# One ring of score row tiles, longer loads, and the first lists made between row tiles, in an argmax, gather and scatter kernel

## The chip, the cores and the metric

One core of a Trainium2 chip. The metric is the time of one execution in microseconds (us), as the device reports it; a profiled execution of the same program has a span some 2 us shorter. All runs quoted here are in the fast state, at full clock.

## The reference

```python
B, S, H = (8, 2048, 2560)          # scores: B x S x S, values: B x S x H, float32
...
best_j   = np.argmax(scores, axis=2)
...
gathered = values[b_idx, best_j, :].copy()
out = np.zeros_like(values)
np.add.at(out, (b_idx, best_j, slice(None)), gathered)
```

For each batch, row j of the output is values[j] times the number of score rows whose largest element is in column j. So only the counts are needed: rows with count 1 are copied, rows with count 0 are zeroed, rows with a higher count are gathered, scaled and scattered. With random scores about 37% are of the first kind, 37% of the second.

## The kernel before

VectorE finds the column of the maximum of every score row (two passes over 128 x 2048 elements, 4.6 us a row tile, 16 row tiles a batch) and turns columns into one-hot tiles from which TensorE makes the counts. From the counts VectorE makes three lists of row numbers. GpSimd issues one indirect transfer per 128 list entries; entries past the end of a list are dropped. SyncE loads the scores, 2 rows per partition (2 MB) at a time:

```python
    R = 2
    ...
    NV = 6                        # staging slots of H elements for the gathered rows
    NX = NV * H // (R * S)        # score tiles of two rows that fit into that room
    NB = 7
    ...
    spool = ctx.enter_context(tc.tile_pool(name="spool", bufs=NB))
    ...
    vbig = ctx.enter_context(nc.sbuf_tensor([P, NV * H], FP32))
...
        for u in range(NT // R):                      # count_steps: one batch of scores
            x = b * NT // R + u
            if x < 2 * (NX + NB) and x % (NX + NB) < NX:
                x %= NX + NB
                s_tile = vbig[:, x * R * S:(x + 1) * R * S]     # early: also in the staging room
            else:
                s_tile = spool.tile([P, R * S], FP32, name="s_tile")[:]
            ...
            for r in range(R):
                ...
                nc.vector.max(out=mx[:], in_=rows)
                nc.vector.max_index(out=am[:, g, :], in_max=mx[:], in_values=rows)
                if g < G - 1:
                    yield
...
        first = 6 if b < 2 else 4                     # value_steps: the lists of one batch
        for t in range(first):
            copy_once(t)
        ...                                           # zero and many lists; three yields in between
        def gathers():
            for k in range(MCAP):
                v = stage()
                gather(v, mi[:, k:k + 1])
                nc.scalar.activation(out=v, in_=v, func=Copy, bias=0.0, scale=mc[:, k:k + 1])
                ...
        ...
        if b == 0:
            zeros(range(nz))          # each zero scatter also issues one of the copies left
            for _ in range(10):
                yield
            gathers()
        else:
            ...
        for k in range(MCAP):
            scatter(staged[k], mi[:, k:k + 1], ...)
...
        for b in range(B):
            for _ in count_steps(b, cnt_ps):
                next(pending, None)   # one step of the lists of the batch before
            ...
            pending = value_steps(b, cnt_ps)
            if b < 2:
                for _ in range(4):    # batches 0 and 1: lists in one go
                    next(pending)
```

Of the kernel before, what the change touches and what calls it, by code (L numbers as in the profile page):

```python
# [8 lines left out]
FP32 = mybir.dt.float32  # L9
# [5 lines left out]
P = 128  # L15
# [21 lines left out]
def kernel(  # L37
# [6 lines left out]
    nc = tc.nc  # L44
    B, S, S2 = scores.shape
    _, _, H = values.shape
    assert S == S2
    NT = S // P
    BIG = float(1 << 24)
    R = 2  # L50
    G = 4
    NV = 6
    NX = NV * H // (R * S)
    NB = 7
    NM = NT // 2
    NE = 16
    LE = P // NE
# [7 lines left out]
    last_row = nc.gpsimd.to_reg(B * S - 1)  # L65

    consts = ctx.enter_context(tc.tile_pool(name="consts", bufs=1))
    spool = ctx.enter_context(tc.tile_pool(name="spool", bufs=NB))
    small = ctx.enter_context(tc.tile_pool(name="small", bufs=3))
    fin = ctx.enter_context(tc.tile_pool(name="fin", bufs=2))  # L70
    ohp = ctx.enter_context(tc.tile_pool(name="ohp", bufs=1))
# [44 lines left out]
    zero1 = consts.tile([P, 1], FP32)  # L116
# [2 lines left out]
    zrow = ctx.enter_context(nc.sbuf_tensor([P, H], FP32))  # L119
    nc.scalar.copy(zrow[:], zero1[:].to_broadcast([P, H]))  # L120

    vbig = ctx.enter_context(nc.sbuf_tensor([P, NV * H], FP32))
    nc.scalar.copy(vbig[:, NX * R * S:NV * H], zero1[:].to_broadcast([P, NV * H - NX * R * S]))

    ones_i = ctx.enter_context(nc.sbuf_tensor([P, B * NT], INT32))
    zero_i = ctx.enter_context(nc.sbuf_tensor([P, B * NT], INT32))
# [30 lines left out]
            in_=v, in_offset=None, bounds_check=B * S - 1, oob_is_err=False))  # L157

    vslot = [0]

    def stage():
        v = vbig[:, vslot[0] * H:(vslot[0] + 1) * H]
        vslot[0] = (vslot[0] + 1) % NV
        return v

    def count_steps(b, cnt_ps):

        am = None
        for u in range(NT // R):
            x = b * NT // R + u  # L170
            if x < 2 * (NX + NB) and x % (NX + NB) < NX:
                x %= NX + NB
                s_tile = vbig[:, x * R * S:(x + 1) * R * S]
            else:
                s_tile = spool.tile([P, R * S], FP32, name="s_tile")[:]
            rows_in = scores[b, u * R * P:(u + 1) * R * P, :].rearrange("(p r) s -> p (r s)", r=R)

            parts = R if b == u == 0 else 1
            for r in range(parts):
                part = slice(r * R * S // parts, (r + 1) * R * S // parts)  # L180
                nc.sync.dma_start(out=s_tile[:, part], in_=rows_in[:, part])
            if u * R % G == 0:
                am = small.tile([P, G, 8], U32, name="am")
            for r in range(R):
                g = (u * R + r) % G
                rows = s_tile[:, r * S:(r + 1) * S]
                mx = small.tile([P, 8], FP32)
                nc.vector.max(out=mx[:], in_=rows)  # L188
                nc.vector.max_index(out=am[:, g, :], in_max=mx[:], in_values=rows)  # L189
                if g < G - 1:  # L190
                    yield
            if (u + 1) * R % G == 0:
                lo = small.tile([P, G], U32)
                nc.vector.tensor_single_scalar(out=lo[:], in_=am[:, :, 0], scalar=P - 1, op=ALU.bitwise_and)  # L194
                hi = small.tile([P, G], U32)
                nc.vector.tensor_single_scalar(out=hi[:], in_=am[:, :, 0], scalar=7, op=ALU.logical_shift_right)  # L196
                oh_lo = small.tile([P, G, P], BF16)
                nc.vector.tensor_tensor(  # L198
                    out=oh_lo[:], in0=lo[:].unsqueeze(2).to_broadcast([P, G, P]),
                    in1=lane_f[:].unsqueeze(1).to_broadcast([P, G, P]), op=ALU.is_equal)  # L200
                oh_hi = small.tile([P, G, NT], BF16)
                nc.vector.tensor_tensor(  # L202
                    out=oh_hi[:], in0=hi[:].unsqueeze(2).to_broadcast([P, G, NT]),
                    in1=lane_f[:, 0:NT].unsqueeze(1).to_broadcast([P, G, NT]), op=ALU.is_equal)
                for g in range(G):
                    t = (u + 1) * R - G + g
                    nc.tensor.matmul(out=cnt_ps[:], lhsT=oh_lo[:, g, :], rhs=oh_hi[:, g, :],  # L207
                                     start=(t == 0), stop=(t == NT - 1))
                yield

    def level_engines(rank):

# [59 lines left out]
    def value_steps(b, cnt_ps):  # L272
# [14 lines left out]
                nc, out_flat[:, :], values[b, t * P:(t + 1) * P, :], one_i[:, t:t + 1], last_row))  # L287


        first = 6 if b < 2 else 4  # L290
        for t in range(first):
            copy_once(t)

# [22 lines left out]
        if b == B - 1:  # L316
# [9 lines left out]
            out=oh[:], in0=lo[:].unsqueeze(2).to_broadcast([P, NT, P]),  # L326
# [4 lines left out]
            out=ez[:], in0=hi[:, 0, :].unsqueeze(2).to_broadcast([P, NT, NT]),  # L331
# [3 lines left out]
            out=em[:], in0=hi[:, 1, :].unsqueeze(2).to_broadcast([P, NT, NM]),  # L335
# [6 lines left out]
        for t in range(NT):  # L342
            nc.tensor.matmul(out=l_ps[:], lhsT=oh[:, t, :], rhs=put[:, t, :], start=(t == 0), stop=(t == NT - 1))  # L343
        yield
        yield

        mi = many_i[:, b * NM:(b + 1) * NM]
        mc = many_c[:, b * NM:(b + 1) * NM]
# [10 lines left out]
# [4 lines that stand above are left out]
                nc.scalar.activation(out=v, in_=v, func=mybir.ActivationFunctionType.Copy, bias=0.0,  # L363
                                     scale=mc[:, k:k + 1])
                staged.append(v)
                if rest:
                    copy_once(rest.pop(0))

        def zeros(columns):
            for k in columns:  # L370
                scatter(zrow[:], zi[:, k:k + 1], free_running)
                if rest:
                    copy_once(rest.pop(0))
# [3 lines left out]
        if b == 0:  # L377
            zeros(range(nz))

            for _ in range(10):  # L380
                yield
            gathers()
        else:
            gathers()
            zeros(range(ZHEAD))
# [9 lines left out]
    with tc.manual_schedule(engines={ET.PE, ET.DVE, ET.Activation, ET.SP}):  # L395
        pending = iter(())
        for b in range(B):
            cnt_ps = psum_c.tile([P, NT], FP32)
            for _ in count_steps(b, cnt_ps):
                next(pending, None)  # L400
            for _ in pending:
                pass
            pending = value_steps(b, cnt_ps)
            if b < 2:
                for _ in range(4):
                    next(pending)
        for _ in pending:
            pass
        full = fin.tile([1, 2], FP32)
        nc.vector.tensor_reduce(out=full[:, 0:1], in_=tots[0:1, 0, 0:B - 1], op=ALU.max, axis=mybir.AxisListType.X)  # L410
        nc.vector.tensor_reduce(out=full[:, 1:2], in_=tots[0:1, 1, :], op=ALU.max, axis=mybir.AxisListType.X)
        over = fin.tile([1, 3], FP32)
        nc.vector.tensor_single_scalar(out=over[:, 0:1], in_=full[:, 0:1], scalar=float(ZCAP * P), op=ALU.is_gt)
        nc.vector.tensor_single_scalar(out=over[:, 1:2], in_=full[:, 1:2], scalar=float(MCAP * P), op=ALU.is_gt)
        nc.vector.tensor_single_scalar(out=over[:, 2:3], in_=most[0:1, :], scalar=float(ZLAST * LE), op=ALU.is_gt)
        over_i = fin.tile([1, 1], INT32)
        nc.vector.tensor_reduce(out=over_i[:], in_=over[:], op=ALU.max, axis=mybir.AxisListType.X)
# [3 lines left out]
    with tc.If(more > 0):  # L421
# [20 lines left out]
        for b in range(B):  # L442
            for k in range(MCAP, NM):
# [3 lines left out]
                with tc.issue_after(last.ins):  # L447
                    scaled = nc.gpsimd.tensor_scalar(
                        out=zrow[:], in0=zrow[:], scalar1=many_c[:, i:i + 1], scalar2=None, op0=ALU.mult)
# [37 lines left out]
```

## Time and profile before

| | before |
|---|---|
| time, median of 3 runs (4 by the time of the comparison) | 828.03 us (828.37) |
| span of the profiled run | 826.9 us |
| bytes moved, of them score loads | 347.04 MB, 134.22 MB |
| VectorE busy, until | 679.3 us, about 700 us |
| mean rate of the transfers over the span | 420 GB/s |
| rate at 90 to 110 us, and at 150 to 171 us | 367 GB/s, 426 GB/s |

The lines to read are in the prediction below. The point of them: VectorE and the DMA engines are both full, but VectorE ends 127 us before the kernel does, so the end is set by bytes over rate. Only time in which the transfers move less than some 427 GB/s can be won. The place aimed at is at 90 to 110 us, when VectorE makes all lists of batch 0 in one go, no score tile comes free, and the load queue runs dry.

### The profile page before, as it was taken

The numbers are of one execution on the slowest core, as the hardware profiler recorded it, in microseconds if no ns is written. First come the engines' busy times: TensorE is split into PE (matmuls) and PEld (weight loads), VectorE is DVE, ScalarE is ACT, GpSimd is POOL, SyncE is SP. The second block draws the span as 40 slices with busy tenths as digits, with TensorE's granted clock in tenths as the row PEclk, the third lists the DMA queues.
The fourth block names the chain that finished last, engine by engine and source line by source line (L and its number), as shares of the span: only waits on it lengthen the run. The fifth ranks groups of instructions, "written<-read, shape, count | busy, mean of one in ns | idle before, by whom it ended". The sixth has DMA issues, their size and how long they took to land.

```text
span 826.9 us, 2079 instructions
## 1 busy us (share of the span) xinstructions
PE 14.7 (2%) x273; PEld 14.2 (2%) x273; DVE 679.3 (82%) x794; ACT 103.0 (12%) x43; POOL 274.1 (33%) x277
## 2 busy tenths in 40 slices
PE   0000000000000000000000000000000000000000
PEld 0000000000000000000000000000000000000000
DVE  7999999999999999999999999999999996000000
ACT  3000000501210001220002300002200220230230
POOL 0000643157021160052330151511425356346442
DMA  9999999999999999999999999999999999999997
GB/s 380 430 426 430 372 423 422 425 411 422 423 425 428 428 427 430 425 427 427 429 424 426 426 430 430 422 429 426 427 426 423 424 427 422 425 424 424 422 427 295
DMA packets 48112, 347.04 MB, mean 420 GB/s; under 512 B 19014, under 2 KB 19014, under 8 KB 19014
## 3 DMA queue, kind: packets, MB, share of 16 engines
q0 software_dynamic: 38736, 212.67, 62.0%
q1 hardware_dynamic: 9360, 134.22, 38.2%
q14 instruction: 14, 0.11, 0.0%
q8 instruction: 2, 0.03, 0.0%
HBM read 354.42 MB, written 300.15 MB: 792 GB/s over the span
## 4 chain that ended last, share of the span: by engine, by line
DVE 43%; DMA 18%; issue 17%; POOL 11%; another core or an unknown queue 8%; PE 0%; POOLq 0%
DVE am L189 19%; DVE mx L188 18%; DMA vbig<-in_values_dram,many_i 14%; POOL out_dram L33 6%; DMA out_dram<-vbig,many_i 4%; POOL out_dram L155 4%; POOL vbig L150 2%; DVE oh_lo L198 1%; DVE oh L325 1%; DMA vbig<-in_scores_dram 1%; DVE lo L194 0%; DVE oh_hi L202 0%; PE l_ps L343 0%; DVE put L340 0%
## 5 line engine op out<-in xcount | busy, mean ns | idle before, releaser
L189 DVE FIND_INDEX8 am<-mx,s_tile 128x8 uint32<-128x2048 f32 x116 | 265.0, 2285 | 0.0
L188 DVE MAX8 mx<-s_tile 128x8 f32<-128x2048 f32 x116 | 264.3, 2278 | 0.0
L363 ACT ACTIVATE vbig<-vbig,many_c 128x2560 f32<-128x2560 f32 x40 | 96.8, 2426 | 692.7 <-DMA vbig<-in_values_dram,many_i 658.5
L33 POOL DMA_INDIRECT out_dram<-in_values_dram,ones_i x128 | 132.3, 1033 | 152.3 <-DVE m L296 114.3
L155 POOL DMA_INDIRECT out_dram<-vbig,many_i x40 | 39.3, 983 | 239.1 <-ACT vbig L363 236.3
L150 POOL DMA_INDIRECT vbig<-in_values_dram,many_i x40 | 41.9, 1048 | 126.8 <-DMA out_dram<-vbig,many_i 79.2
L155 POOL DMA_INDIRECT out_dram<-zrow,zero_i x61 | 59.5, 976 | 18.8 <-issue 18.8
L188 DVE MAX8 mx<-vbig 128x8 f32<-128x2048 f32 x12 | 27.3, 2279 | 4.8 <-DMA vbig<-in_scores_dram 4.8
L189 DVE FIND_INDEX8 am<-mx,vbig 128x8 uint32<-128x2048 f32 x12 | 27.4, 2284 | 0.0
L198 DVE TENSOR_TENSOR oh_lo<-lo,lane_f 128x512 bf16<-128x512 uint32 x32 | 22.3, 696 | 0.4
L325 DVE TENSOR_TENSOR oh<-lo,fill_f 128x2048 f16<-128x2048 uint32 x8 | 18.3, 2292 | 0.3
L207 PE MATMUL cnt_ps<-oh_hi,oh_lo 128*128 128x16 bf16 x128 | 8.2, 174 | 579.0 <-DVE oh_hi L202 529.4
L207 PEld LDWEIGHTS <-oh_lo 128*128 128x128 bf16 x128 | 8.4, 105 | 578.8 <-DVE oh_lo L198 577.8
L189 DVE MATCH_VALUE_LOAD am<-mx,s_tile 128x8 f32 x116 | 10.7, 92 | 4.0
L202 DVE TENSOR_TENSOR oh_hi<-hi,lane_f 128x64 bf16<-128x64 uint32 x32 | 7.0, 217 | 0.0
L194 DVE TENSOR_SCALAR lo<-am 128x4 uint32<-128x4 uint32 x32 | 5.8, 181 | 1.1
L343 PE MATMUL l_ps<-put,oh 128*128 128x32 f16 x128 | 4.7, 188 | 68.8 <-DVE put L340 68.8
L343 PEld LDWEIGHTS <-oh 128*128 128x128 f16 x128 | 4.7, 104 | 69.9 <-DVE oh L325 59.6
L196 DVE TENSOR_SCALAR hi<-am 128x4 uint32<-128x4 uint32 x32 | 5.4, 170 | 0.0
L351 DVE TENSOR_SCALAR e<-l_ps 128x32 f32<-128x32 f32 x8 | 1.5, 187 | 3.1 <-PE l_ps L343 3.1
L330 DVE TENSOR_TENSOR ez<-hi,lane_f 128x256 f16<-128x256 uint32 x8 | 3.3, 418 | 0.0
L340 DVE TENSOR_TENSOR put<-ez,row_f 128x256 f16<-128x256 f16 x8 | 3.3, 417 | 0.0
(91 smaller groups left out, 61.3 us busy)
## 6 DMA issues: line engine op xcount, KB each, us to landing
s_tile<-in_scores_dram SPq DMA_DIRECT2D x58, 2048.0 KB, 12.0
vbig<-in_scores_dram SPq DMA_DIRECT2D x5, 2048.0 KB, 37.3
vbig<-in_scores_dram SPq DMA_DIRECT2D x2, 1024.0 KB
out_dram<-in_values_dram,ones_i POOLq DMA_INDIRECT x128
out_dram<-zrow,zero_i POOLq DMA_INDIRECT x61
vbig<-in_values_dram,many_i POOLq DMA_INDIRECT x40, 33.0
out_dram<-vbig,many_i POOLq DMA_INDIRECT x40, 59.1
```

What stands on the lines that cost most here:

```text
L33: return eng.add_instruction(ins)
L150: note(nc.gpsimd.indirect_dma_start(out=v, out_offset=None, in_=values_flat[:, :], in_offset=bass.IndirectOffsetOnAxis(ap=idx, axis=0), bo ...
L155: note(nc.gpsimd.indirect_dma_start(out=out_flat[:, :], out_offset=bass.IndirectOffsetOnAxis(ap=idx, axis=0), in_=v, in_offset=None, bound ...
L188: nc.vector.max(out=mx[:], in_=rows)
L189: nc.vector.max_index(out=am[:, g, :], in_max=mx[:], in_values=rows)
L194: nc.vector.tensor_single_scalar(out=lo[:], in_=am[:, :, 0], scalar=P - 1, op=ALU.bitwise_and)
L198: nc.vector.tensor_tensor(out=oh_lo[:], in0=lo[:].unsqueeze(2).to_broadcast([P, G, P]), in1=lane_f[:].unsqueeze(1).to_broadcast([P, G, P]) ...
L202: nc.vector.tensor_tensor(out=oh_hi[:], in0=hi[:].unsqueeze(2).to_broadcast([P, G, NT]), in1=lane_f[:, 0:NT].unsqueeze(1).to_broadcast([P, ...
L207: nc.tensor.matmul(out=cnt_ps[:], lhsT=oh_lo[:, g, :], rhs=oh_hi[:, g, :], start=(t == 0), stop=(t == NT - 1))
L325: nc.vector.tensor_tensor(out=oh[:], in0=lo[:].unsqueeze(2).to_broadcast([P, NT, P]), in1=fill_f[:].unsqueeze(1).to_broadcast([P, NT, P]), ...
L343: nc.tensor.matmul(out=l_ps[:], lhsT=oh[:, t, :], rhs=put[:, t, :], start=(t == 0), stop=(t == NT - 1))
L363: nc.scalar.activation(out=v, in_=v, func=mybir.ActivationFunctionType.Copy, bias=0.0, scale=mc[:, k:k + 1])
```

## The change

Its intent: keep the transfers full around the first lists. All score tiles become single row tiles in one room (7 in the staging room for the first two turns, 14 behind it, 21 where there were 20). Loads take up to 4 rows per partition where places lie side by side, 1 row for tiles 36 to 41, 2 rows for tiles 42 to 63. For batch 0, only the list of single rows is made at once, all 16 copies are issued first, and the other lists are made between row tiles of batch 1.

```diff
-    R = 2
+    R = 4
...
-    NX = NV * H // (R * S)
-    NB = 7
+    NX = NV * H // S
+    NB = 14
...
+    room = ctx.enter_context(nc.sbuf_tensor([P, NV * H + NB * S], FP32))
...
+    turn = NX + NB
...
+    def place(x):
+        return NV * H + (x % turn - NX if x < 2 * turn else (x - 2 * turn) % NB) * S
...
+    while x < B * NT:
+        n = 1
+        most_n = 1 if x < 2 or 2 * turn - 6 <= x < 2 * turn else 2 if x < 4 or 2 * turn <= x < 4 * NT else R
+        while n < most_n and (x + n) % NT and place(x + n) == place(x) + n * S:
+            n += 1
+        loads[x] = n
+        x += n
...
-        for u in range(NT // R):
...
+        for t in range(NT):
+            x = b * NT + t
+            if x in loads:
+                n = loads[x]
+                nc.sync.dma_start(out=room[:, place(x):place(x) + n * S], in_=...)
...
-        first = 6 if b < 2 else 4
+        first = (NT, 6, 4)[min(b, 2)]
...
         yield
-        yield
+        if b > 0:
+            yield
...
-            for _ in range(10):
+            while tiles[0] < turn + NX:
                 yield
...
...
-            if b < 2:
-                for _ in range(4):
-                    next(pending)
+            for _ in range((1, 4, 0)[min(b, 2)]):
+                next(pending)
```

More of the change, by code (lines that the diff above doesn't have):

```diff
@@ L67 @@
     consts = ctx.enter_context(tc.tile_pool(name="consts", bufs=1))
-    spool = ctx.enter_context(tc.tile_pool(name="spool", bufs=NB))
     small = ctx.enter_context(tc.tile_pool(name="small", bufs=3))
@@ L120 @@
     nc.scalar.copy(zrow[:], zero1[:].to_broadcast([P, H]))
-    vbig = ctx.enter_context(nc.sbuf_tensor([P, NV * H], FP32))
-    nc.scalar.copy(vbig[:, NX * R * S:NV * H], zero1[:].to_broadcast([P, NV * H - NX * R * S]))
+    room = ctx.enter_context(nc.sbuf_tensor([P, NV * H + NB * S], FP32))
+    nc.scalar.copy(room[:, 0:NV * H - NX * S], zero1[:].to_broadcast([P, NV * H - NX * S]))
+    turn = NX + NB
+    def place(x):
+        return NV * H + (x % turn - NX if x < 2 * turn else (x - 2 * turn) % NB) * S
+    loads, x = {}, 0
+    while x < B * NT:
[5 more added lines that the diff above has]
+        x += n
     ones_i = ctx.enter_context(nc.sbuf_tensor([P, B * NT], INT32))
@@ L159 @@
     vslot = [0]
+    tiles = [0]
     def stage():
-        v = vbig[:, vslot[0] * H:(vslot[0] + 1) * H]
+        v = room[:, vslot[0] * H:(vslot[0] + 1) * H]
         vslot[0] = (vslot[0] + 1) % NV
@@ L168, in count_steps @@
         am = None
-        for u in range(NT // R):
-            x = b * NT // R + u
-            if x < 2 * (NX + NB) and x % (NX + NB) < NX:
-                x %= NX + NB
-                s_tile = vbig[:, x * R * S:(x + 1) * R * S]
-            else:
-                s_tile = spool.tile([P, R * S], FP32, name="s_tile")[:]
-            rows_in = scores[b, u * R * P:(u + 1) * R * P, :].rearrange("(p r) s -> p (r s)", r=R)
-            parts = R if b == u == 0 else 1
-            for r in range(parts):
-                part = slice(r * R * S // parts, (r + 1) * R * S // parts)
-                nc.sync.dma_start(out=s_tile[:, part], in_=rows_in[:, part])
-            if u * R % G == 0:
-                am = small.tile([P, G, 8], U32, name="am")
-            for r in range(R):
-                g = (u * R + r) % G
-                rows = s_tile[:, r * S:(r + 1) * S]
-                mx = small.tile([P, 8], FP32)
-                nc.vector.max(out=mx[:], in_=rows)
-                nc.vector.max_index(out=am[:, g, :], in_max=mx[:], in_values=rows)
-                if g < G - 1:
-                    yield
-            if (u + 1) * R % G == 0:
+        for t in range(NT):
+            x = b * NT + t
+            if x in loads:
+                n = loads[x]
+                nc.sync.dma_start(out=room[:, place(x):place(x) + n * S],
+                                  in_=scores[b, t * P:(t + n) * P, :].rearrange("(p r) s -> p (r s)", r=n))
+            g = t % G
+            if g == 0:
+                am = small.tile([P, G, 8], U32, name="am")
+            rows = room[:, place(x):place(x) + S]
+            mx = small.tile([P, 8], FP32)
+            nc.vector.max(out=mx[:], in_=rows)
+            nc.vector.max_index(out=am[:, g, :], in_max=mx[:], in_values=rows)
+            if g == G - 1:
                 lo = small.tile([P, G], U32)
@@ L204, in count_steps @@
                     in1=lane_f[:, 0:NT].unsqueeze(1).to_broadcast([P, G, NT]), op=ALU.is_equal)
-                for g in range(G):
-                    t = (u + 1) * R - G + g
-                    nc.tensor.matmul(out=cnt_ps[:], lhsT=oh_lo[:, g, :], rhs=oh_hi[:, g, :],
-                                     start=(t == 0), stop=(t == NT - 1))
-                yield
+                for k in range(G):
+                    nc.tensor.matmul(out=cnt_ps[:], lhsT=oh_lo[:, k, :], rhs=oh_hi[:, k, :],
+                                     start=(t == G - 1 and k == 0), stop=(t == NT - 1 and k == G - 1))
+            tiles[0] = x + 1
+            yield
     def level_engines(rank):
@@ L344, in value_steps @@
         yield
-        yield
+        if b > 0:
+            yield
         mi = many_i[:, b * NM:(b + 1) * NM]
```

## The prediction

> **What bounds the kernel now.** I read the page from its top: engine shares first, then the strip of slices.
>
> ```profile
> PE 14.7 (2%) x273; PEld 14.2 (2%) x273; DVE 679.3 (82%) x794; ACT 103.0 (12%) x43; POOL 274.1 (33%) x277
> ...
> DVE  7999999999999999999999999999999996000000
> ...
> DMA  9999999999999999999999999999999999999997
> ```
>
> Two things are full at once. VectorE runs without a break until about 700 us and then stops; the 16 DMA engines are in the top band in every slice but the last. So I asked what is left after VectorE has ended, and what the queues moved in all.
>
> ```profile
> DMA packets 48112, 347.04 MB, mean 420 GB/s; under 512 B 19014, under 2 KB 19014, under 8 KB 19014
> ...
> q0 software_dynamic: 38736, 212.67, 62.0%
> q1 hardware_dynamic: 9360, 134.22, 38.2%
> ```
>
> The score loads (q1) are 134.22 MB; the GpSimd transfers (q0: copies of rows that occur once, zero rows, gathers and scatters of rows that occur often) are 212.67 MB. After 700 us only q0 is left, at full speed: from 700 to 810 us it moved 46.68 MB at 424 GB/s and a DMA share of 1.01 to 1.03. A batch has 212.67/8 = 26.6 MB of such work, so when VectorE ends nearly two batches of it are in arrears. A VectorE that ended earlier would therefore not end the kernel earlier: the transfer engines set the time. The chain of waits starts with VectorE (am and mx, 37%) because it follows the last release at each step; it does not show that the transfers were full meanwhile.
>
> The end is thus bytes over rate, plus what the DMA engines lost. At the 427 GB/s of 300 to 600 us, 347.04 MB take 812.7 us; the span is 826.9, so 14.2 us are lost. Where, the table of 10 us stretches shows (last two columns: DMA share, GB/s; before those the engines' busy time):
>
> ```profile
> 0.00:10.00 10.00, 0.00 (x0) 0.00 (x0) 4.34 (x8) 6.26 (x3) 1.09 (x8) 1.00 0.84 329
> 80.00:90.00 10.00, 0.45 (x6) 0.39 (x6) 9.24 (x27) 0.00 (x0) 3.36 (x3) 1.00 1.01 429
> 90.00:100.00 10.00, 0.59 (x16) 0.58 (x16) 8.87 (x14) 0.00 (x0) 7.87 (x8) 1.00 0.93 325
> 100.00:110.00 10.00, 0.00 (x0) 0.00 (x0) 9.90 (x9) 0.00 (x0) 7.56 (x9) 1.00 1.01 409
> 180.00:190.00 10.00, 0.00 (x0) 0.00 (x0) 9.93 (x7) 0.00 (x0) 7.56 (x9) 1.00 1.01 386
> 810.00:820.00 10.00, 0.00 (x0) 0.00 (x0) 0.00 (x0) 0.00 (x0) 1.50 (x2) 1.00 0.95 390
> 820.00:830.00 10.00, 0.00 (x0) 0.00 (x0) 0.00 (x0) 0.00 (x0) 0.00 (x0) 1.00 0.16 56
> ```
>
> In time at 427 GB/s: the start 2.3 us (10 x (1 - 329/427)), the hole at 90 to 110 us 2.8 us (2.4 + 0.4), the dip at 180 about 1.0, the end (4.45 MB in the last 16.9 us, which need 10.4) 6.5 us. These make 12.6 of the 14.2 us; the rest is spread thin.
>
> The hole is what the change aims at. At 84 us the counts of batch 0 are ready; VectorE then makes all lists of batch 0 in one go, from 84.9 to 93.2 us, with the 2.29 us one-hot tile and a 1.02 us wait for PE in it, and finishes no score tile. The load queue waits for exactly that:
>
> ```profile
> SPq L181 <- DVE am L189: 45.8, 4, 18.6
> SPq L181 <- DVE hi L196: 29.5, 4, 9.0
> ```
>
> (time in all up to 110 us, times, longest). The longest, 18.6 us, is the load of rows 36 and 37, which needs both row tiles 16 and 17: 93.2 us plus two tiles of 4.6 us is 102.4, and the next load is issued at 102.8. What was queued ran dry at about 92 us: q1 has 26 packets in 90 to 100 us. Meanwhile q0 had six copies, one each 1.28 us, of which only some 37% of the 128 rows are moved (128 copies of 128 rows for a share of rows of 1/e under random counts: about 0.48 MB each, an estimate), so 0.48/1.28 = 376 GB/s at most.
>
> **What the Trainium skill says.** "DMA: Bandwidth & Descriptors", section "Where 436 GB/s comes from", puts the ceiling at 435.2 GB/s. The trace agrees: score loads alone, 10 to 80 us, ran at 429 GB/s, 98.5% of it, so there is no faster stage to be had. Its section "Issuing engines are not separate DMA queues" says that transfers of all issuers interleave on the same 16 engines; agreed, the shares 62.0% and 38.2% add to 100%. Its section "Queues, rings and completion order" says that each engine takes turns among its queues packet by packet; a bigger packet would give the score queue a larger turn. No run here shows it yet. Its section "Why small descriptors are slow" names a fixed cost per packet. My own reading from the trace: alone, a 16 KB score packet took 16 x 70 / 1831 = 612 ns (2055 packets less 224 small ones), and a 10 KB row in the tail 16 x 110 / 4557 = 386 ns. The slope is 226 ns for 6144 B, 27.2 GB/s per engine, leaving about 10 ns per packet.
>
> **The change, part by part.** No arithmetic goes: the VectorE program has 653 rows in both builds, GpSimd issues the same kinds and numbers of transfers, and the bytes are the same.
>
> *Loads.* Before: 65 loads (63 of 2 rows, 2 of 1), 65 x 128 = 8320 data packets, plus 16 small ones each, the 9360 of the page. After, worked from the code: 48 loads (20 of 4, one of 3, 18 of 2, 9 of 1). The 4-row form is not only late: tiles 4 to 35 have it (with one of 1 and one of 3), then six of 1, eleven of 2 up to tile 63, then 4 and 2. Packets are 48 x 144 = 6912. 17 x 128 = 2176 data packets saved x 10.4 ns / 16 engines = 1.4 us.
>
> *Start.* The first two loads are 1 row as before, so the first wait of VectorE (4.8 us) stays. At 2.45 us per row tile (1.05 MB at 429), tiles 4 to 7 land as one at 5.9 + 7 x 2.45 = 23 us; VectorE took its fifth tile at 26.2. No new wait. Ring of 21: tiles 21 to 24 need tiles 0 to 3 (done at 25), 32 to 35 need tile 14 (done at 78.9) and the queue would run dry at 5.9 + 31 x 2.45 = 81.8; tight but enough. Tile 36 needs 15, done at 83.5, dry at about 91.6.
>
> *The hole.* After: at 84 us VectorE makes only the list of single rows (to the first yield, 1.9 us), then tile 16, then the big lists, then tile 17. Tile 37 can be loaded once 16 is done, at about 91.5, and no longer needs 17. GpSimd has 16 copies to issue at once, 86 to 106.6 us, then 7 zero scatters. So q0 gets 376 GB/s of work and q1 at least a row tile per 5 to 10 us on top, more than 427 together. Lost bytes come back: at most 2.8 us. But of that only 0.7 us is idle share (0.93 in ten us); the rest is slow packets, since the copies carry many dropped rows (585 small q0 packets in 90 to 100 us), and those must be processed whenever they come. I count 2.0.
>
> *Later for batch 0.* Gathers need the value room free: before from 122.1 us (row tile 21), now from tile 22 on, about 127 us. By 115.6 us q0 will have been given 16 x 0.48 + 7 x 1.03 = 14.9 MB and can't have drained more than some 8 of it. No gap. VectorE saves about 1 us of PE wait, which is worth nothing at the end.
>
> *Batch 1 and the tail.* The four steps at once remain for batch 1, so the dip at 180 stays; the last batch and the 6.5 us of the end are untouched.
>
> *Against it.* Four-row loads come every 19 us or more and leave q0 alone between. q0 alone ran at 424, mixed 427: 0.7% over some 60 us of more separate running is 0.4 us.
>
> Sum: 828.0 - 2.0 - 1.4 + 0.4 = 825.0 us.
>
> **Rivals.** (a) *VectorE starves on big loads.* A ring of 14 with 4 in flight leaves 10 tiles, 46 us of VectorE work; a 2 MB load beside q0 took 12.0 us to land, so 4 MB some 24. Even if a few waits of 5 us came, the arrears of q0 at 700 us would absorb them. Time: 825 to 827. (b) *Bigger turns of the score queue starve q0*, so that scaled rows come late and GpSimd's chain is longer. For it: gathers took 33.0 us to land, scatters 59.1, and GpSimd waited 236 us on ACT. Against it: loads are paced by VectorE, so their share over 20 us can't grow. If gaps of 1 us came in each of six batches: 829 to 831. (c) *The hole is only displaced*: sixteen thin copies in a row are processed at the same slow rate, or tile 38 is late instead. Then only the packets count: 826.5 to 828. (d) *Longer packets stream better than my 10 ns*: with 20 ns, 822 to 823.
>
> **Range and chances.** (c) and (b) set the high end, (d) with the whole hole returned (828.0 - 2.8 - 2.8 = 822.4) and some thin losses repaired the low end: 820.5 to 828.5. Two per cent are 16.6 us, more than all losses together (14.2 us), so faster by that is nearly excluded; slower would need 7 MB of new idle time where 50 MB of arrears stand by.
>
> **What would show it.** Right: at 90 to 110 us over 415 GB/s, no load wait of 18 us; 6912 q1 packets and q1's share down to about 38.0%; VectorE still ending near 700; a tail after 810 as before. Wrong: a DMA share under 0.95 somewhere between 110 and 800 us (GpSimd's chain), waits of VectorE on score loads beyond the first, or a rate in score-only stretches well off 429 (longer packets behave otherwise).

## The result

| | before | changed |
|---|---|---|
| time, median (4 runs each) | 828.37 us | 827.43 us |
| changed over before | | 0.9988, 95% interval 0.9971 to 1.0005 |
| span of the profiled run | 826.9 us | 825.6 us |
| packets on the load queue | 9360 | 6912 |

It is inside the predicted range, but the forecast gain of 3.0 us came out as 0.9 us. A second set of five runs (label d3_changed_again below) gave 0.9986, interval 0.9973 to 0.9999, so a gain of some 1 us is likely real. Ratios here are the mean time of one kernel's fast runs over that of the other's of the same rounds, so they are not quite the ratio of the medians. As the kernel before varies by about 1 us from set to set, kernels are compared below by their ratios to it, multiplied by 828.

The pages of the changed kernel that answer to the first lines in the prediction:

```profile
DVE  7999999999999999999999999999999996000000
...
DMA  9999999999999999999999999999999999999997
...
q0 software_dynamic: 38736, 212.67, 62.1%
q1 hardware_dynamic: 6912, 134.22, 38.1%
```

Packets and bytes are as worked out (q0 is GpSimd's queue, q1 the load queue). Nothing in the strips tells the two kernels apart. The table of stretches does (last two columns: DMA share, GB/s). First the kernel before:

```profile
90.00:110.00 20.00, 0.59 (x16) 0.58 (x16) 18.77 (x22) 0.00 (x0) 15.43 (x16) 1.00 0.97 367
110.00:150.00 40.00, 0.51 (x8) 0.53 (x8) 39.66 (x33) 4.43 (x2) 11.85 (x12) 1.00 1.01 424
150.00:171.00 21.00, 0.25 (x4) 0.26 (x4) 20.76 (x21) 7.71 (x4) 3.90 (x4) 1.00 1.02 426
171.00:200.00 29.00, 1.31 (x26) 1.24 (x26) 27.07 (x47) 0.64 (x1) 21.67 (x20) 1.00 1.01 410
```

and the changed kernel:

```profile
90.00:110.00 20.00, 0.59 (x16) 0.58 (x16) 19.68 (x27) 0.00 (x0) 15.74 (x15) 1.00 1.01 398
110.00:150.00 40.00, 0.51 (x8) 0.52 (x8) 39.62 (x37) 0.00 (x0) 10.77 (x11) 1.00 1.01 423
150.00:171.00 21.00, 0.50 (x8) 0.52 (x8) 20.35 (x25) 12.03 (x5) 4.88 (x5) 1.00 0.97 385
171.00:200.00 29.00, 1.05 (x22) 0.97 (x22) 27.52 (x41) 0.00 (x0) 22.52 (x21) 1.00 1.01 409
```

The hole is mended in part (367 to 398 GB/s, where the prediction asked for over 415) and a new one stands at 150 to 171 us (426 to 385). The best reading of this is a ledger: the bytes that each kernel has moved from the start up to a moment. The view of the transfers with a window from 0 gives them. Before, up to 110 us, then up to 171 us:

```profile
DMA packets 4157, 44.93 MB, mean 408 GB/s; under 512 B 1061, under 2 KB 1061, under 8 KB 1061
...
DMA packets 7736, 70.83 MB, mean 414 GB/s; under 512 B 2375, under 2 KB 2375, under 8 KB 2375
```

The changed kernel at the same two moments:

```profile
DMA packets 3568, 45.73 MB, mean 416 GB/s; under 512 B 1171, under 2 KB 1171, under 8 KB 1171
...
DMA packets 7146, 70.72 MB, mean 414 GB/s; under 512 B 2314, under 2 KB 2314, under 8 KB 2314
```

At 110 us the changed kernel is 0.80 MB ahead, 1.9 us at 427 GB/s and almost the 2.0 us that I had counted. At 171 us it is 0.11 MB behind. Three more profiles, of kernels that load and list batch 0 as the changed one does (d3 and c2 with the same program up to then, a1 with shorter loads), repeat this against the one profile of the kernel before: 0.76 to 0.89 MB ahead at 110 us, between 0.13 MB behind and 0.03 MB ahead at 171 us (e1, the same up to 114 us, is only 0.38 MB ahead at 110 us). What stood still at 150 to 171 us is seen in the waits of the changed kernel in that window, first of the engines, then of the load queue:

```profile
POOL out_dram L170 <- ACT room L370: 15.6, 5, 8.1
...
SPq L189 <- DVE am L197: 43.1, 1, 43.1
SPq L189 <- DVE hi L202: 9.0, 1, 9.0
```

The load queue had waited 43.1 us for VectorE to release a row tile: the 7 places of the staging room have left the ring, so the load of tiles 42 and 43 needs tiles 28 and 29, and it is issued at 159.4 us. The kernel before has such a pause too, of 38.8 us; but with 20 places for score tiles it had loaded 40 tiles by then where the changed kernel had loaded 42, and it starts again earlier, at 150.6 us. GpSimd has issued everything that batch 0 has to give but five scatters, each of which waits for ScalarE to scale its rows, which waits for a gather to land. The gathers were issued from 121.3 to 144.8 us, each when VectorE had released its slot. The lists of batch 1 come at 171.1 us:

```profile
153.84 1.00 POOL L170 DMA_INDIRECT out_dram<-room,many_i  x1 [8.08 <-ACT room L370]
156.83 0.99 POOL L170 DMA_INDIRECT out_dram<-room,many_i  x1 [1.99 <-ACT room L370]
159.87 0.96 POOL L170 DMA_INDIRECT out_dram<-room,many_i  x1 [2.05 <-ACT room L370]
162.95 0.97 POOL L170 DMA_INDIRECT out_dram<-room,many_i  x1 [2.11 <-ACT room L370]
165.27 0.97 POOL L170 DMA_INDIRECT out_dram<-room,many_i  x1 [1.35 <-ACT room L370]
171.08 0.98 POOL L33 DMA_INDIRECT out_dram<-in_values_dram,ones_i  x1 [4.85 <-DVE m L302]
```

(Start, us, instruction; in brackets the idle time before it and what ended it.) The kernel before was 0.75 MB behind at 150 us (61.89 against 62.64 MB), so it still had that work to do in this stretch, and its loads were issued at 150.6 and 160.8 us. The view of the transfers at 150 to 171 us (packets, MB, share of 16 engines) shows where the difference lies, before and then changed:

```profile
q0 software_dynamic: 667, 4.92, 55.8%
q1 hardware_dynamic: 261, 4.01, 45.7%
...
q0 software_dynamic: 766, 5.97, 69.3%
q1 hardware_dynamic: 140, 2.10, 27.2%
```

The load queue moved 1.91 MB less, GpSimd's queue 1.05 MB more, in all 0.86 MB less.

So the theory at this point, called D below: until the lists of batch 1 come, there is only so much to move, the 26.5 MB of batch 0 and the score tiles that the ring lets in; what is moved earlier is missing later. Its rivals: the order of GpSimd's issues makes the gap, not the supply (G); as to the length of the packets, each packet costs some 10 ns (P), packets cost nothing (Q), or the 4-row loads even hurt (R).

### The profile page after: what moved, and what is told of

Read it like the earlier page. It is cut to its first block, busy times and chain, and to the rows that moved or that the text cites. A ratio compares the mean times of both kernels' runs of the same rounds, so it can differ in the third digit from the quotient of the medians.

```text
span 825.6 us, 2045 instructions
## 1 busy us (share of the span) xinstructions
PE 14.7 (2%) x273; PEld 14.1 (2%) x273; DVE 679.0 (82%) x794; ACT 101.2 (12%) x43; POOL 274.7 (33%) x277
## 3 DMA queue, kind: packets, MB, share of 16 engines
q1 hardware_dynamic: 6912, 134.22, 38.1%
## 4 chain that ended last, share of the span: by engine, by line
DVE 71%; DMA 13%; issue 8%; POOL 5%; another core or an unknown queue 1%; POOLq 0%; PE 0%; DVEq 0%
DVE am L197 32%; DVE mx L196 30%; DMA room<-in_values_dram,many_i 8%; DMA out_dram<-room,many_i 4%; POOL out_dram L33 2%; DVE oh_lo L204 2%; POOL out_dram L170 2%; DVE oh L331 2%; POOL room L165 1%; DMA room<-in_scores_dram 1%; DVE lo L200 1%; DVE oh_hi L208 0%; DVE hi L202 0%; DVE put L346 0%
## 5 line engine op out<-in xcount | busy, mean ns | idle before, releaser
L196 DVE MAX8 mx<-room 128x8 f32<-128x2048 f32 x128 | 291.7, 2279 | 4.6 <-DMA room<-in_scores_dram 4.6
L197 DVE FIND_INDEX8 am<-mx,room 128x8 uint32<-128x2048 f32 x128 | 292.4, 2285 | 0.0
L370 ACT ACTIVATE room<-room,many_c 128x2560 f32<-128x2560 f32 x40 | 96.7, 2426 | 693.0 <-DMA room<-in_values_dram,many_i 693.0
L170 POOL DMA_INDIRECT out_dram<-room,many_i x40 | 39.7, 994 | 248.2 <-ACT room L370 248.2
L165 POOL DMA_INDIRECT room<-in_values_dram,many_i x40 | 41.8, 1046 | 122.2 <-DMA out_dram<-room,many_i 73.9
L197 DVE MATCH_VALUE_LOAD am<-mx,room 128x8 f32 x128 | 11.8, 92 | 4.3
L321 DVE TENSOR_SCALAR rank<-base,off_ps 128x16 f32<-128x16 f32 x16 | 3.2, 244 | 0.0
L344 DVE TENSOR_TENSOR put<-em,row_f 128x128 f16<-128x128 f16 x8 | 2.4, 298 | 0.3
```

The costliest lines, as they stand in the source:

```text
L165: note(nc.gpsimd.indirect_dma_start(out=v, out_offset=None, in_=values_flat[:, :], in_offset=bass.IndirectOffsetOnAxis(ap=idx, axis=0), bo ...
L170: note(nc.gpsimd.indirect_dma_start(out=out_flat[:, :], out_offset=bass.IndirectOffsetOnAxis(ap=idx, axis=0), in_=v, in_offset=None, bound ...
L370: nc.scalar.activation(out=v, in_=v, func=mybir.ActivationFunctionType.Copy, bias=0.0, scale=mc[:, k:k + 1])
```

## The experiments

Sets of kernels ran on one chip each, in the same rounds with the kernel before. The ledger of the main ones, in MB moved from the start up to the moment named, read from the same view:

| up to, us | before | changed | again (d3) | a3 | d1 | d2 | d4 | b1 | b2 | e1 | e2 | a2 |
|---|---|---|---|---|---|---|---|---|---|---|---|---|
| 86 | 35.89 | 36.12 | 36.15 | 36.09 | 35.99 | 36.09 | 36.12 | 36.15 | 35.89 | 35.99 | 36.05 | 35.33 |
| 110 | 44.93 | 45.73 | 45.82 | 45.64 | 45.05 | 44.68 | 46.11 | 46.20 | 45.05 | 45.31 | 45.61 | 45.32 |
| 150 | 61.89 | 62.64 | 62.77 | 62.62 | 62.05 | 61.15 | 63.05 | 63.00 | 61.90 | 62.40 | 61.84 | 62.39 |
| 171 | 70.83 | 70.72 | 70.82 | 70.93 | 70.79 | 69.57 | 71.13 | 72.03 | 70.90 | 71.15 | 70.18 | 70.35 |
| 700 | 295.89 | 295.99 | 296.16 | 295.87 | 295.77 | 294.66 | 296.16 | 297.39 | 296.36 | 296.20 | 295.00 | 295.03 |

0.1 MB is 0.23 us. Two profiles of the same kernel (changed and d3) differ by 0.03 to 0.17 MB in this table; e1, whose program is the same up to 114 us, has 0.42 MB less by 110 us than the changed kernel. So a single entry is good to some 0.1 to 0.4 MB, and I lean on differences that stay over several rows or agree with the times.

### a1_two_rows and a2_one_row: what a packet costs

```diff
-        most_n = 1 if x < 2 or 2 * turn - 6 <= x < 2 * turn else 2 if x < 4 or 2 * turn <= x < 4 * NT else R
+        most_n = 1 if x < 2 or 2 * turn - 6 <= x < 2 * turn else 2      # a1_two_rows
+        most_n = 1                                                      # a2_one_row
```

> The changed kernel, but no load of more than 2 rows per partition (one condition cut; ring, order of lists and everything else as changed). About 1340 of its data packets are split in two again. Theory P (each packet costs some 10 ns of its DMA engine, as predicted): 0.9 us slower than the changed kernel, about 828.3. Theory Q (longer packets gave nothing, the whole 0.9 us came from elsewhere): same as the changed kernel, 827.4. Theory R (4-row loads hurt, coming in bursts): faster than it.

> The changed kernel with every load of 1 row per partition: 128 loads, 18432 packets on the load queue in place of 6912, 11520 more (10240 data, 1280 small). This measures the packet cost with a long lever. Theory P (10.4 ns per data packet, 16 engines): 10240 x 10.4 / 16 = 6.7 us slower, about 834. Theory Q (cost hidden): within 1.5 us of 827.4.

a1: 828.73 us, ratio 0.9996 (0.9982 to 1.0010), with 9936 load packets. It is 0.0008 x 828 = 0.7 us above the changed kernel, close to theory P, but the interval is wider than that. a2 has the longer lever: 832.14 us, ratio 1.0035 (1.0021 to 1.0048), 18432 packets. That is (1.0035 - 0.9988) x 828 = 3.9 us for 11520 more packets, 3.9 x 16 / 11520 = 5.4 ns for each. Theory Q (no cost) and R (long loads hurt) are out; P is right in kind, with about half the size at the end: 5.4 ns in place of 10.4.

The traces say where the other half goes, though these are single profiles. Where the score queue runs alone, at 10 to 80 us, its packets took 312, 612, 916 and 1213 ns (medians of the packet records in a2, the kernel before, and for the last two the changed kernel) for 8, 16, 24 and 32 KB: 300 ns for each 8 KB and some 12 ns that do not grow with size. So the prediction's 10.4 ns is about right there. In the mixed stretches less of it is lost. The stretches of the changed kernel and then of a2:

```profile
10.00:80.00 70.00, 0.76 (x12) 0.78 (x12) 69.45 (x65) 0.00 (x0) 0.00 (x0) 1.00 1.01 433
300.00:600.00 300.00, 6.21 (x114) 6.07 (x114) 296.15 (x319) 36.30 (x15) 88.91 (x88) 1.00 1.01 428
...
10.00:80.00 70.00, 0.76 (x12) 0.78 (x12) 69.45 (x65) 0.00 (x0) 0.00 (x0) 1.00 1.01 422
300.00:600.00 300.00, 6.21 (x114) 6.05 (x114) 296.21 (x319) 36.42 (x15) 80.03 (x79) 1.00 1.01 426
```

At 300 to 600 us a2 moves 0.67 MB less (127.70 against 128.37), 1.6 us at 427 GB/s for 6138 more packets, an estimate of 4 ns each. And of its 0.79 MB arrears at 86 us, 0.41 are left at 110 us and 0.37 at 171 us: what fewer packets save early is mostly gone by the end of the same gap.

Packet size does not delay the gathers either, which was rival (b) of the prediction: from the issue of the first gather to the first scaling it takes 29.8 us in the changed kernel, 30.2 in a1 and 30.8 in a2.

### a3_lists_at_once: only the order of the lists undone

```diff
-        first = (NT, 6, 4)[min(b, 2)]
+        first = 6 if b < 2 else 4
-        if b > 0:
-            yield
+        yield
-            for _ in range((1, 4, 0)[min(b, 2)]):
+            for _ in range((4, 4, 0)[min(b, 2)]):
```

> The changed kernel with the lists of batch 0 made in one go again and 6 copies first, as before; loads and ring as changed. The hole at 90 to 110 us comes back. Theory D (the hole was only displaced: until the lists of batch 1 come, the transfers have no more bytes to move than the 26.6 MB of batch 0 and the score tiles that the ring lets in, so what is moved earlier is missing at 150 to 171 us): within 0.7 us of 827.4, with the gap at 150 to 170 us smaller than in the changed kernel. The prediction's step (2 us come back with the hole): 829.4 or more.

828.35 us, ratio 0.9992 (0.9979 to 1.0006): 0.3 to 0.5 us above the changed kernel, within the 0.7 us of theory D. But the hole did not come back: 397 GB/s at 90 to 110 us, 45.64 MB by 110 us. That part of my expectation was wrong. The loads fill the hole, whatever the order of the lists: with tiles 36 to 41 loaded one by one, tile 36 needs only tile 15 and is issued at 83.2 us, and the next at 97.2 and 101.8 us; the kernel before had to wait for a pair until 102.5 us.

### c1_five_slots: one more ring tile

```diff
-    NV = 6
-    NB = 14
+    NV = 5
+    NB = 15
```

> The changed kernel with 5 staging slots in place of 6 and 15 ring tiles in place of 14 (21 in the first turns as now). One more score tile, 1.05 MB, may be let in before the lists of batch 1 come, and the room for the gathers is free one row tile (4.6 us) earlier. Theory D (supply before 171 us is what limits there): over 410 GB/s at 150 to 170 us (390 and 373 in the changed kernel) and 1 to 2.5 us faster, about 825.5. Rival G (the gap comes from the order in which GpSimd issues, not from the supply): gap unchanged, 827.4; and slower, 828 to 832, if five slots make the later gathers wait more than the transfers' arrears cover.

829.05 us, ratio 1.0002 (0.9989 to 1.0016), not faster. The load after the long pause is issued at 154.9 in place of 159.4 us, but 150 to 171 us has 389 GB/s and 70.81 MB are moved by 171 us. The expectation of theory D failed; a gap that stays and a time of 828 to 832 us is what rival G had said of five slots. With five slots the last scaled scatters went out at 164.7 and 169.8 us in place of 163.0 and 165.3. My reading is that what the load queue brought forward, the chain of gather, scaling and scatter lost; no run separates the two.

### c2_batch1_steps: the lists of batch 1 between row tiles too

```diff
-        first = (NT, 6, 4)[min(b, 2)]
+        first = (NT, NT, 4)[min(b, 2)]
-        if b > 0:
+        if b > 1:
             yield
-            for _ in range((1, 4, 0)[min(b, 2)]):
+            for _ in range((1, 1, 0)[min(b, 2)]):
```

> The changed kernel with the lists of batch 1 also made between row tiles, and all 16 copies of batch 1 first. It goes after the dip at 180 to 200 us (393 and 409 GB/s, 1.2 us at 427). Theory D says that after 171 us the supply is larger than what can be moved, so a gap filled there is kept: 0.5 to 1.5 us faster than the changed kernel, 826 to 827. Rival S (those stretches are slow because copies with many dropped rows are slow, not because work is missing): no gain, 827.4, slow stretch moved or longer.

829.49 us, ratio 1.0011 (0.9997 to 1.0024), 1.9 us above the changed kernel. 171 to 200 us ran at 400 GB/s (409 in the changed kernel), with a DMA share of 1.01 in both. This is what rival S says: the stretch is slow because of what is in it, not because work is missing, and it is slower with sixteen thin copies in a row. It accounts for part of the loss only: up to 700 us c2 is 0.28 MB behind the changed kernel (295.71 against 295.99), 0.7 us.

### b1_after_half and b2_before_half: VectorE done with batch 1 much earlier

Wrong results: in batch 1, even row tiles are searched only in columns 0 to 1023, odd ones only from 1024 on. b2 has the same edit in the kernel before.

```diff
+            if b == 1:
+                rows = room[:, place(x) + t % 2 * S // 2:place(x) + (t % 2 + 1) * S // 2]
             nc.vector.max(out=mx[:], in_=rows)
             nc.vector.max_index(out=am[:, g, :], in_max=mx[:], in_values=rows)
...
+                if b == 1:
+                    nc.vector.tensor_scalar_add(hi[:, 1:G:2], hi[:, 1:G:2], NT / 2.0)
```

> Wrong results on purpose. The changed kernel in which VectorE searches only half the columns in batch 1 (first half for even row tiles, second half for odd ones), so that its 16 tiles take about 37 us less and the lists of batch 1 come at about 135 us in place of 171; bytes of that batch 26.42 MB in place of 26.62. Theory D: the transfers have work early enough, the gap at 150 to 170 us closes and the filled hole at 90 to 110 us is kept as gain: 825.0 to 825.5, and 2.3 to 3.5 us faster than the kernel before with the same edit. Rival G (the gap is due to the GpSimd order, or the gain is lost elsewhere): 827 and only 1 us faster than that one.

> Wrong results on purpose. The kernel before with the same edit (batch 1 searched in half its columns, 26.58 MB). It keeps the hole at 90 to 110 us. Theory D: the hole is now a real loss, because later arrears come earlier: 827.5 to 828.3, that is 2.3 to 3.5 us slower than the changed kernel with this edit (0.4 us of that from the 0.16 MB of other rows). Rival G: 1 us slower than it.

b1: 825.67 us, ratio 0.9963 (0.9949 to 0.9977). b2: 827.97 us, ratio 0.9990 (0.9977 to 1.0003). They are (0.9990 - 0.9963) x 828 = 2.2 us apart, where the unedited pair is 1.0 us apart; 0.4 us of it are other bytes, as worked out beforehand. With an interval of 0.0014 (1.2 us) to each side of either ratio, 1.8 against 1.0 us is not clear of noise, so the reading rests on the bytes. The stretches of b1 and then of b2:

```profile
90.00:110.00 20.00, 0.84 (x20) 0.84 (x20) 19.62 (x34) 0.00 (x0) 15.73 (x15) 1.00 1.02 422
110.00:150.00 40.00, 1.56 (x30) 1.50 (x30) 38.04 (x76) 0.00 (x0) 9.86 (x11) 1.00 1.02 420
150.00:171.00 21.00, 0.26 (x4) 0.26 (x4) 20.79 (x19) 2.43 (x1) 0.99 (x1) 1.00 1.01 430
```

```profile
90.00:110.00 20.00, 0.85 (x20) 0.85 (x20) 18.97 (x34) 0.00 (x0) 15.43 (x16) 1.00 0.98 374
110.00:150.00 40.00, 1.56 (x30) 1.49 (x30) 38.01 (x77) 0.00 (x0) 10.80 (x11) 1.00 1.01 421
150.00:171.00 21.00, 0.25 (x4) 0.26 (x4) 20.83 (x18) 3.80 (x2) 1.00 (x1) 1.00 1.02 429
```

With no gap at 150 to 171 us, the lead is kept: b1 leads b2 by 1.15 MB at 110 us, by 1.13 MB at 171 us and still by 1.03 MB at 700 us. In the unedited pair 0.80 MB become -0.11 MB. The size in time is a little under what I expected (2.3 to 3.5 us).

Two limits. First, it was not the lists of batch 1 that closed the gap. VectorE began them early, at 137 us, but in the program's order GpSimd's copies of batch 1 stand behind the scaled scatters of batch 0: the first one was issued at 190.5 us in b1 and 192.8 in b2, later than the 171.1 us of the changed kernel. What came earlier were score loads, as VectorE released row tiles sooner: b1 issues them at 130.0, 134.9, 153.6 and 162.7 us, the changed kernel only at 159.4 and 168.6, and at 150 to 171 us the load queue moves 3.64 MB in b1 against 2.10. So this pair does not test the "until the lists of batch 1 come" of theory D. What it tests is an earlier return of the load queue.

Second, the lead did not become time in the two executions that were profiled: b1 still leads by 1.06 MB at 810 us (2.5 us), yet they end at 824.4 and 824.9 us. GpSimd's last issues lie at 806.0 and 805.8 us, so they ended no sooner in b1. The medians are further apart than these two executions; why is open.

### d1_no_singles_at_once and d2_no_singles: what fills the hole, and what a hole costs

```diff
-        most_n = 1 if x < 2 or 2 * turn - 6 <= x < 2 * turn else 2 if x < 4 or 2 * turn <= x < 4 * NT else R
+        most_n = 1 if x < 2 else 2 if x < 4 or 2 * turn <= x < 4 * NT else R     # d1 (with a3's edit) and d2
```

> The changed kernel once more, so that the runs of this set have it in their own rounds. 0.998 to 0.9995 of the kernel before if the first figure (0.9988) holds.

> The changed kernel with the lists of batch 0 in one go, and without the rule that row tiles 36 to 41 are loaded one by one (they come as 4 and 2). The run with only the lists undone still filled the hole at 90 to 110 us (397 GB/s), so the loads must fill it. If the single loads do: the hole is back, under 380 GB/s at 90 to 110 us and under 45.1 MB moved by 110 us. Theory D then says that it costs little all the same: 70.6 to 71.0 MB moved by 171 us as in every kernel so far, and a time within 0.7 us of the changed kernel. If holes do cost: 2 us slower, 829.5.

> Only the rule of the single loads for tiles 36 to 41 undone; lists of batch 0 between row tiles as changed. If lists between tiles are enough to fill the hole, as predicted: over 395 GB/s at 90 to 110 us. If the single loads are what does it: under 380. Theory D: within 0.7 us of the changed kernel either way, 70.6 to 71.0 MB by 171 us.

d3: 827.38 us, ratio 0.9986. d1: 828.33 us, ratio 0.9995 (0.9982 to 1.0008). The hole is back in d1 (368 GB/s, 45.05 MB by 110 us), 150 to 171 us is nearly full again (416 GB/s), 70.79 MB are moved by 171 us, and the time is 0.0009 x 828 = 0.7 us above the changed kernel:

```profile
90.00:110.00 20.00, 0.58 (x16) 0.58 (x16) 19.12 (x22) 0.00 (x0) 15.43 (x16) 1.00 0.97 368
150.00:171.00 21.00, 0.36 (x8) 0.47 (x8) 20.60 (x21) 9.60 (x4) 4.88 (x5) 1.00 1.01 416
```

So the single loads fill the hole: with them it runs at 397 and 398 GB/s in either order of the lists (a3, changed), without them at 368 and 347 (d1, d2). What filling it is worth is not clear of noise, as the intervals overlap: d1 is 0.7 us above the changed kernel, from which it also differs by the order of the lists and 576 load packets fewer, and 0.2 us above a3, from which it differs by the single loads alone (0.9995 against 0.9992, from two sets).

d2: 831.18 us, ratio 1.0027 (1.0015 to 1.0039), 3.4 us above the changed kernel. This is a miss for theory D in the form in which I had put it.

```profile
90.00:110.00 20.00, 0.59 (x16) 0.58 (x16) 19.68 (x27) 0.00 (x0) 15.73 (x15) 1.00 0.96 347
110.00:150.00 40.00, 0.51 (x8) 0.53 (x8) 39.62 (x37) 0.00 (x0) 10.68 (x11) 1.00 0.99 412
150.00:171.00 21.00, 0.51 (x8) 0.52 (x8) 20.35 (x25) 12.03 (x5) 4.86 (x5) 1.00 1.00 401
```

With the lists between row tiles, GpSimd has nothing but thin copies to issue until 107 us, and with the loads in fours SyncE issues none between 78.6 and 105.6 us. By 110 us d2 is 1.05 MB behind the changed kernel; by 171 us it is 1.15 MB behind, and by 700 us 1.33 MB. My reading is that a hole is made good later only if the later stretch has room, and here that stretch is itself thin. Against d1, which has the same loads and ran in the same rounds, d2 is (1.0027 - 0.9995) x 828 = 2.6 us slower: the order of the lists, which I had taken for the cure, is harmful without the single loads.

### d4_two_tiles_half: VectorE done with batch 1 a little earlier

Wrong results: the edit of b1, for the first two row tiles of batch 1 alone.

> Wrong results on purpose. The changed kernel with only the first two row tiles of batch 1 searched in half their columns, so that the lists of batch 1 come some 4.5 us earlier (166.5 us in place of 171); 26.53 MB in that batch in place of 26.62, 0.2 us. Theory D (all that is there has been moved by the time these lists come, so each us earlier is one us at the end, until the gap of about 2 us is used up): 1.5 to 2.3 us faster than the changed kernel, as much as with all 16 tiles halved. Rival G: 0.2 to 0.5 us faster.

826.68 us, ratio 0.9976 (0.9963 to 0.9989): 0.8 us faster than the changed kernel, 0.2 us of which are bytes. That is between D (1.5 to 2.3) and G (0.2 to 0.5), and its interval overlaps that of d3. 71.13 MB are moved by 171 us, but 150 to 171 us still has 385 GB/s. The run does not test what it was made for. VectorE wrote the first list of batch 1 at 166.5 us, but GpSimd waited for ScalarE with the last scaled scatter until 169.8 us and issued the first copy of batch 1 at 172.3 us, later than the changed kernel (171.1). Only the score loads came earlier, at 155.2 and 164.4 us in place of 159.4 and 168.6. So it decides nothing between D and G, but shows the chain of gather, scaling and scatter holding up work that was there.

### e1_hold_two and e2_hold_four: work that waits for nothing, kept for the thin stretch

In the changed kernel 24.56 MB of GpSimd's transfers are moved by 171 us, and batch 0 has 26.5 MB (748 rows copied, 761 zeroed, 539 gathered and scattered, of 10240 B each). About 1.9 MB are there, but behind the chain. Theory E: that chain makes the stretch thin, and other work, kept back, would fill it.

```diff
-            zeros(range(nz))
+            zeros(range(nz - HOLD))          # HOLD = 2 (e1), 4 (e2)
...
         for k in range(MCAP):
+            if b == 0 and k < HOLD:
+                zeros([nz - HOLD + k])
             scatter(staged[k], ...)
```

> The changed kernel, but the last two of the seven zero scatters of batch 0 (of which only one moves rows, 1.24 MB; batch 0 has 761 empty rows) are issued after the gathers, between the scatters of the scaled rows, so at about 146 and 154 us in place of 115. Theory E (at 150 to 171 us the transfers are thin because what is left of batch 0 sits behind gather, scaling and scatter; work that waits for nothing fills it): over 405 GB/s at 150 to 171 us (385 in the changed kernel), 71.1 MB or more by 171 us (70.7), and 1 to 2 us faster, about 826. Theory D (by 171 us there is nothing more to move in any order): 70.6 to 70.9 MB by 171 us and within 0.5 us of the changed kernel.

> The same with four zero scatters held back (3.9 MB). Theory E: 150 to 171 us is full, over 415 GB/s, but about 2 MB are missing at 116 to 150 us (423 GB/s in the changed kernel), where the score loads pause; no better than the changed kernel, 827 to 829. Theory D: the same 70.6 to 70.9 MB by 171 us, 827.4.

e1: 827.43 us, ratio 0.9985 (0.9971 to 0.9998). The stretch fills (417 GB/s against 385) and 71.15 MB are moved by 171 us, both as theory E says and against D: work that waits for nothing does fill it. But the time is that of the changed kernel: the lead of 0.33 MB over d3 at 171 us is 0.04 MB at 700 us. Why it melts is open. e2: 831.39 us, ratio 1.0034 (1.0020 to 1.0047): with 3.9 MB kept back, 130 to 150 us falls to 390 GB/s and 150 to 171 us to 397; E had this in kind, and the loss is larger than expected.

Of all versions with right results none is clearly faster than the changed kernel.

## Why the prediction was wrong

The sum was 828.0 - 2.0 (hole) - 1.4 (packets) + 0.4 (loads in bursts) = 825.0. Measured: 827.4, a gain of 0.9 to 1.2 us.

- **What bounds the kernel** was right in the main. VectorE ends at 699 us before and 697 us changed, long before the kernel does. But bytes over rate does not carry the last stage: at 810 us the changed kernel leads by only 0.13 MB (0.3 us), and its profile ends 1.3 us earlier, with GpSimd's last issue at 809.2 in place of 810.8 us.
- **The step that failed** is "Later for batch 0. [...] No gap." I checked that GpSimd's queue would still have bytes at 127 us, when I thought the gathers would start, and stopped there. They start at 121.3 us, as the first staging slot needs row tile 21 alone; but the gap is some 25 us after my 127, at 150 to 171 us: 385 GB/s against 426 before, with a DMA share of 0.93 at 150 to 160 us, a sign of being wrong that the prediction had named itself (under 0.95). There the load queue, which has two tiles more behind it, is let in 8.8 us later than before and moves 1.91 MB less, and GpSimd's last scatters sit behind gather and scaling. What was won by 110 us (0.80 MB) is gone by 171 us. Shown by the ledger of four profiles against that of the kernel before; and by b1 and b2, where the load queue is let in earlier, the gap is absent and the lead in bytes stays to 810 us. What the gap cost in time is not clear of noise in any pair.
- **The hole, -2.0 us.** The size of the repair was right (0.80 MB, 1.9 us), though one sign was not met: 398 GB/s at 90 to 110 us, not over 415, as 100 to 110 us has 388 at a DMA share of 1.02, with thin copies in it. Its worth at the end was 0.2 to 0.7 us by d1, not clear of noise. I had listed "the hole is only displaced" as a rival with 826.5 to 828; that is what happened, through the later gap more than through the slow copies that I gave as its reason.
- **What fills the hole.** I named both the order of the lists and the single loads. a3 and d1 show that it is the single loads (tiles 36 to 41); d2 shows that the order without them makes things worse, by 2.6 us against d1.
- **Packets, -1.4 us.** Right in kind, mis-sized: 2448 packets fewer x 5.4 ns / 16 = 0.8 us. The 10.4 ns themselves were about right (12 ns, between packets of one queue in one stretch). What failed is that I let every packet of the run count in full: where the queues mix it is about 4 ns, and what was saved early is in part lost in the gap. This term alone would account for the result within its interval; how much of the 1 us lies in the last 15 us of the run is not settled.
- **Loads in bursts, +0.4 us.** No run shows it: a1, with loads of at most 2 rows, is no faster than the changed kernel.
- **The test "no load wait of 18 us"** was a bad one: the changed kernel has waits of 19.0 and 19.3 us up to 110 us, before the hole, while loads issued earlier were still landing. They cost nothing to speak of: 10 to 80 us ran at 433 GB/s.
- **Not settled**: how the two limits share the gap at 150 to 171 us (the supply of score tiles, as the load queue's 1.91 MB and b1 suggest, or the chain, as e1 and d4 show), why e1's lead melts, and why that of b1 does in the last 15 us of its profile. No run puts the load queue's pause right in a kernel with right results and leaves the chain as it is.

## What to carry to other kernels

Where the transfers set the end, keep a ledger of bytes moved from the start up to several moments for both kernels: a mended hole is a gain only if the lead is still there at the last moment, and the end itself can still lose it (b1). After closing a gap, look for the next moment at which all queues wait on the same slow producer, and ask whether the work moved forward was what filled that moment before. In a ring that feeds such queues, the size of the load at the tight moment (one tile or two or four) decides when it may start, and here mattered more than the order of the compute. When an edit is meant to bring a step forward, check in the trace that the step did come forward: in b1, b2 and d4 it did not.

## What the Trainium skill lacked or had wrong

- "DMA: Bandwidth & Descriptors": its section "Where 436 GB/s comes from" says that for transfers between HBM and SBUF the HBM side of about 358 GB/s binds, beside a measured 425 of its own; the condition, both cores of a pair streaming, stands only beside the measurements further up on the page. Here, with one core in use, score loads alone ran at 429 GB/s at 10 to 80 us in the kernel before and 433 in the changed one. Its section on small descriptors works the fixed cost of a packet out for 256 bytes, in cycles; it has no time for packets of 8 KB and more. Here these took some 12 ns beyond what grows with size (312 ns for 8 KB, 612 for 16, 1213 for 32), and 11520 packets more, of 8 KB in place of mostly 16 and 32 KB, cost 3.9 us at the end, 5.4 ns each on 16 engines.
- "Perfetto Trace Analysis", section "Identifying the Most-Contended Engine", does say to judge the transfers by HBM utilization (bytes moved) rather than occupancy, but gives no example of how far the two part. Here 100 to 110 us of the changed kernel has a DMA share of 1.02 at 388 GB/s, 180 to 190 us 1.03 at 393, and 700 to 810 us 1.02 at 425.
- No page gives a time for issuing an indirect transfer. Here 128 list entries mostly took 0.98 us on GpSimd plus 0.30 us to the next, 1.28 us, whether 37% or nearly all of the rows were moved. For the copies that limits the supply to about 376 GB/s, an estimate from the prediction's 0.48 MB a copy.
